# A feed-forward block's DRAM traffic split over two queues, with one operand stored already split

## The chip, the cores and the metric

The kernel runs on one core of one Trainium2 chip. The metric is the time of one execution on the device in microseconds (us). A core has five engines with an instruction list each: TensorE (in the profile PE, its weight loads PEld) multiplies matrices, VectorE (DVE) and ScalarE (ACT) work elementwise, GpSimd (POOL) does small work, and SyncE (SP) here only starts transfers. A transfer is put on the list of the engine that starts it; each list is worked through in its order, and all transfers run on the core's 16 DMA engines.

## The reference

Two layers over a sequence of 1024 tokens of width 1024, batch 1. Layer 0 is a retention and gated delta-net mixer, layer 1 a gated linear recurrence. After each mixer stands the feed-forward block that the change is about:

```
def conv_ffn(hn, w_up, conv_w, conv_b, w_down):      # hn: 1024 x 1024
    up = causal_dwconv(hn @ w_up, conv_w) + conv_b    # w_up: 1024 x 5632, 3 taps
    gate, val = jnp.split(up, 2, axis=-1)             # 2816 columns each
    return (jax.nn.silu(gate) * val) @ w_down         # w_down: 2816 x 1024
...
    h = h + conv_ffn(rms_norm(h, norm_ffn[layer]), ffn_w_up[layer], ffn_conv_w[layer],
                     ffn_conv_b[layer], ffn_w_down[layer])
```

Everything is in float32.

## The kernel before

Activations lie with channels on the 128 partitions and time along them. A float32 product is made of three matmuls (`mm3`, lines 319 to 321): each operand is split into a rounded part `hi` and a rest `lo`, and hi x hi, hi x lo and lo x hi are added up in PSUM. To split costs one ScalarE copy (`hi`) and one VectorE subtraction (`lo`).

The two large products of the feed-forward block use a two-by-two block scheme with seven products where the plain way has eight. `pair_product` makes product `o` (0 to 6) of a pair of output tiles from `kk` slices, three matmuls a slice: 12 matmuls for `kk` = 4. The seven right-hand operands are sums and differences of the blocks of the activations; I call them sets 0 to 6. The seven products share three PSUM banks (`BANK = "ACACABA"`), and after each product a VectorE addition reads the bank (`pair_sums` in the up projection, `pair_added`, line 820, in the down projection, where it adds to the residual `H`).

**Up projection.** 22 hidden tiles `p`, one after the other, each seven products against the sets of the block's input, which lie in `operand(0)` to `operand(6)`. When tile `p`'s products are done, `gate` and `hidden` convolve, gate and multiply on ScalarE and VectorE (lines 850, 852, 936, 941); the result `y` goes through `store_parts`. The hidden tiles fall into groups `c` = 0, 1, 2 of 8, 8 and 6 (`third`, true in layer 0 alone, says that the third group is treated like the others; in layer 1 tiles 16 to 21 are multiplied in the plain way by `final`). `store_parts` makes what the down projection needs from the tile: blocks that are operands as they are, and differences of blocks (`t1` to `t4`). A set in `whole[c]` is split at once (lines 877, 878) and goes to `p_dram` (in the profile `pf_dram`) as `hi` and `lo`; the others go to `s_dram` (`sf_dram`) raw.

**Down projection.** For each group `c` four tiles `t` of seven products. `load_set(c, o)` brings set `o` back into the place of an operand that is no longer used: a set of `whole[c]` in 2 `kk` transfers of 256 KB (line 914), a raw one in `kk` transfers (line 922) into half tiles taken in turn from `room[c]`, each then copied (line 924) and subtracted (line 925). `room[c]` has eight halves, of the buffer `R` and of three `t` tiles. The pool of `t` tiles has three buffers, so `room` waits until the last up tile's `t` tiles have been stored. Group 0's sets take the places of the up projection's operands, so set `o` can start when product `o` of the last up tile (21) is done: `after(21, o)` calls `load_set(0, o)`. Group 1's sets are fetched during the last tile of group 0 (`following`), group 2's during the last tile of group 1. Tile 21's own `hidden` comes after the third down tile of group 0.

The order on each engine is made by a planner from program order, its cost estimates and what waits for what; TensorE's order is fixed by hand only for the first two up tiles. Weights stream through SP too (line 292) into `raw` buffers and are split (lines 272, 273) as they are used.

Of the kernel before, what the change touches and what calls it, by code (L numbers as in the profile page):

```python
# [16 lines left out]
ALU = mybir.AluOpType  # L17
# [6 lines left out]
HALF = 512  # L24
# [65 lines left out]
def f32(ap):  # L90
    return ap.bitcast(F32)
# [12 lines left out]
class Block:  # L104
# [708 lines left out]
    def pair_added(self, t):  # L813

        V = self.nc.vector
        h = lambda i, j: self.H[2 * t + i].rearrange("p (h n c) -> p h n c", h=2, n=2)[:, :, j, :]
        to = ((0, 0), (1, 1), (0, 1), (0, 1), (1, 1), (0, 0), (1, 0))

        def sums(o, ps):
            V.tensor_tensor(h(*to[o]), ps.rearrange("p (h c) -> p h c", c=256), h(*to[o]), ALU.add)  # L820
        return sums

    def ffn(self, layer, gain):
        nc, I = self.nc, self.I
        V, A = nc.vector, nc.scalar
        third = gain is not None
        sets = 3 if third else 2
        y_dram = self.tc.dram_tile([NPAIR, P, T], F32, name=f"yf_dram{layer}")
        s_dram = self.tc.dram_tile([sets, 5, 4, P, HALF], F32, name=f"sf_dram{layer}")

        p_dram = self.tc.dram_tile([sets, 4, 4, 2, P, HALF], F32, name=f"pf_dram{layer}")
        if not third:
            l_dram = self.tc.dram_tile([NPAIR - 16, 2, P, T], F32, name=f"lf_dram{layer}")
        depth = lambda c: 4 if c < 2 else 3

        def where(c, o):

            if c == 0 or not third:
                return self.operand(o)
            if c == 1:  # L840
                return self.operand((o + 3) % 7)
            if o < 3:
                i = (20, 14, 26)[o]
                return self.slots1(i, 6).rearrange("p (s n c) -> p n s c", n=2, c=256)
            return self.s2[:, :, 6 * (o - 3):6 * (o - 2), :]
# [14 lines left out]
        whole = [{0: 0, 1: 1, 3: 2}] + 2 * [{0: 0, 1: 1, 3: 2, 5: 3}]  # L860
        room, loads = {}, [0, 0, 0]

        def store_parts(p, y, hi):

            hi = hi.bitcast(F32R)
            lo = self.parts.tile([P, T], F32R, tag="lo", name="lo")
            if p >= 16 and not third:
                self.split_half(y, (hi, lo))
                for e, t in enumerate((hi, lo)):
                    nc.sync.dma_start(l_dram[p - 16, e], f32(t))  # L870
                return
            c, k = divmod(p, 8)
            kk = depth(c)
            first = slice(0, HALF)

            def store_split(o, src, at):
                A.copy(halves(hi[:, at]), src)  # L877
                V.tensor_tensor(halves(lo[:, at]), src, f32(halves(hi[:, at])), ALU.subtract)  # L878
                for e, t in enumerate((hi, lo)):
                    nc.sync.dma_start(p_dram[c, whole[c][o], k % kk, e], f32(t[:, at]))  # L880
            store = lambda o, r: nc.sync.dma_start(s_dram[c, place[o], k % kk], r)
            sub = lambda out, a, b: V.tensor_tensor(halves(out), a, b, ALU.subtract)  # L882
# [10 lines left out]
            t4 = t3  # L893
            nc.sync.dma_start(halves(t3), blocks(y_dram[p - kk])[:, :, 1])
            nc.sync.dma_start(t2, s_dram[c, place[1], k - kk])
# [5 lines left out]
            sub(t4, v[:, :, 0], halves(t2))  # L901
            store(6, t4)
            if 5 in whole[c]:
                store_split(5, v[:, :, 0], slice(HALF, T))
            else:
                nc.sync.dma_start(halves(s_dram[c, place[5], k % kk]), v[:, :, 0])

        def load_set(c, o):

            x, kk = where(c, o), depth(c)  # L910
            if o in whole[c]:
                for k in range(kk):
                    for e in range(2):
                        nc.sync.dma_start(f32(x[:, :, kk * e + k, :]), halves(p_dram[c, whole[c][o], k, e]))
                return
            if c not in room:
                ts = [self.R] + [self.t() for _ in range(3)][::-1]
                room[c] = [t[:, i * HALF:(i + 1) * HALF] for i in range(2) for t in ts]
            for k in range(kk):
                r = room[c][loads[c] % 8]  # L920
                loads[c] += 1
                nc.sync.dma_start(r, s_dram[c, place[o], k])
                hi, lo = (x[:, :, e + k, :] for e in (0, kk))
                A.copy(hi, halves(r))
                V.tensor_tensor(lo, halves(r), f32(hi), ALU.subtract)  # L925
# [22 lines left out]
        def after(p, o):  # L948
            if p < NPAIR - 1:
                if o == 5:  # L950
                    tgs[p] = gate(p)
            elif o:
                for q in (0, 1) if o == 1 else (o,):
                    load_set(0, q)


        with self.tc.manual_schedule(engines={mybir.EngineType.PE}):
# [1005 lines left out]
```

## Time and profile before

| | |
|---|---|
| median of 3 runs | 2143.78 us (2143.31 to 2144.47) |
| the profiled execution | 2145.08 us, its span 2143.2 us |
| granted TensorE clock | 0.999 |
| instructions | 29749 |
| DMA moved | 313.23 MB, mean 146 GB/s |
| queue q1 (hardware; SP's transfers) | 304.15 MB, 42.5% of 16 engines |
| queue q0 (the transfers that GpSimd starts) | 0.81 MB, 0.2% |
| layer 0's feed-forward block | from about 575 to 1204 us, the down projection from about 985 |

Instructions are grouped by line of the kernel and by tile (`out<-in`, buffer numbers left out). A releaser behind `<-` is what ended an engine's idle time. Matmuls are pipelined: each is given from its start to its modelled end, and consecutive ones overlap. `SPq` rows are the issues of transfers on SP's list; how long a transfer takes to land is given apart. GpSimd's own issues are rows of POOL.

### The profile page before, as it was taken

The numbers are of one execution on the slowest core, as the hardware profiler recorded it, in microseconds if no ns is written. First come the engines' busy times: TensorE is split into PE (matmuls) and PEld (weight loads), VectorE is DVE, ScalarE is ACT, GpSimd is POOL, SyncE is SP. The second block draws the span as 40 slices with busy tenths as digits, with TensorE's granted clock in tenths as the row PEclk, the third lists the DMA queues.
The fourth block names the chain that finished last, engine by engine and source line by source line (L and its number), as shares of the span: only waits on it lengthen the run. The fifth ranks groups of instructions, "written<-read, shape, count | busy, mean of one in ns | idle before, by whom it ended". The sixth has DMA issues, their size and how long they took to land.

```text
span 2143.2 us, 29749 instructions
## 1 busy us (share of the span) xinstructions
PE 2127.4 (99%) x10648; PEld 1771.9 (83%) x10648; DVE 1722.2 (80%) x2630; ACT 1077.3 (50%) x1750; POOL 100.5 (5%) x115
## 2 busy tenths in 40 slices
PE   9999999999999999999999999999999999999998
PEld 7878888888888888887888888888888888888887
DVE  7995677776998989988868786768999889878645
ACT  6444423135665555555324576756655555554222
POOL 0102122300000000000000000000000000000002
PEclk9999999999999999999999999999999999999999
DMA  5354433543145435448745212142354445375542
GB/s 188 91 170 126 136 94 94 172 142 118 46 172 178 160 137 179 172 172 289 233 161 172 72 57 80 64 158 65 123 186 163 149 151 177 118 262 183 182 169 85
DMA packets 242021, 313.23 MB, mean 146 GB/s; under 512 B 62432, under 2 KB 129424, under 8 KB 241872
## 3 DMA queue, kind: packets, MB, share of 16 engines
q1 hardware_dynamic: 205632, 304.15, 42.5%
q10 hardware_dynamic: 35088, 6.36, 1.5%
q8 instruction: 84, 1.38, 0.3%
q0 software_dynamic: 1152, 0.81, 0.2%
q14 instruction: 65, 0.53, 0.1%
HBM read 215.79 MB, written 95.45 MB: 145 GB/s over the span
## 4 chain that ended last, share of the span: by engine, by line
PE 63%; issue 30%; DVE 3%; DMA 2%; POOL 1%; SPq 0%; ACT 0%; POOLq 0%; DVEq 0%
PE ps L319 19%; PE ps L320 18%; PE ps L321 18%; PE pc L319 1%; PE pc L321 1%; PE pc L320 1%; DMA s<-pf_dram 1%; DMA t<-sf_dram 0%; DVE wlo L273 0%; DVE l L1416 0%; DVE l L1418 0%; DVE h L1387 0%; PE pc L1551 0%; PE ps L1595 0%; PE pc L1663 0%
## 5 line engine op out<-in xcount | busy, mean ns | idle before, releaser
L319 PE MATMUL ps<-s,whi 128*128 128x512 f32 (+1 forms) x2692 | 1049.1, 391 | 1.5 <-DVE h L820 0.9
L320 PE MATMUL ps<-s,whi 128*128 128x512 f32 (+1 forms) x2692 | 1044.1, 388 | 2.1 <-DVE s L925 1.9
L321 PE MATMUL ps<-s,wlo 128*128 128x512 f32 (+1 forms) x2692 | 1042.7, 388 | 0.6 <-DVE wlo L273 0.6
L272 ACT CAST whi<-raw 128x512 fp32r<-128x512 f32 (+2 forms) x616 | 374.1, 613 | 611.9 <-PE ps L320 471.6
L319 PEld LDWEIGHTS ps<-s,whi 128*128 128x128 f32 x2692 | 505.8, 188 | 107.0 <-ACT whi L272 1.6
L320 PEld LDWEIGHTS ps<-s,whi 128*128 128x128 f32 x2692 | 505.9, 188 | 106.1 <-DVE s L925 4.6
L321 PEld LDWEIGHTS ps<-s,wlo 128*128 128x128 f32 x2692 | 505.6, 188 | 104.5 <-DVE wlo L273 1.4
L273 DVE TENSOR_TENSOR wlo<-raw,whi 128x512 fp32r<-128x512 f32 (+2 forms) x616 | 415.0, 680 | 50.8 <-ACT whi L272 42.3
L852 DVE SCALAR_TENSOR_TENSOR t<-halo,cols,t 128x1024 f32<-128x1024 f32 x176 | 221.6, 1281 | 2.4 <-ACT t L850 1.0
L820 DVE TENSOR_TENSOR h<-ps,h 128x512 f32<-128x512 f32 x140 | 96.3, 689 | 75.7 <-PE ps L321 75.5
L810 DVE TENSOR_TENSOR halo<-ps,kept 128x512 f32<-128x512 f32 (+1 forms) x138 | 91.8, 666 | 71.1 <-PE ps L321 70.5
L850 ACT ACTIVATE t<-halo,cols 128x1024 f32<-128x1024 f32 x88 | 109.5, 1247 | 18.0 <-DVE halo L810 9.0
L805 ACT COPY kept<-ps 128x512 f32<-128x512 f32 (+1 forms) x138 | 77.0, 558 | 11.0 <-PE ps L321 9.6
L472 POOL TENSOR_TENSOR rtok<-rtok,npow 128x4 f32<-128x4 f32 (+1 forms) x10 | 9.9, 990 | 1097.2 <-DVE rtok L471 1097.2
L877 ACT CAST t<-t 128x512 fp32r<-128x512 f32 x68 | 41.2, 621 | 39.1 <-DVE t L941 37.1
L941 DVE TENSOR_TENSOR t<-t 128x1024 f32<-128x1024 f32 x44 | 53.6, 1219 | 0.0
L553 DVE TENSOR_TENSOR h<-ps,h 128x512 f32<-128x512 f32 (+1 forms) x48 | 28.6, 599 | 30.6 <-PE ps L321 30.5
L882 DVE TENSOR_TENSOR t<-t 128x512 f32<-128x512 f32 x76 | 52.1, 686 | 0.6 <-DMA sf_dram<-t 0.6
L936 ACT ACTIVATE t<-t 128x1024 f32<-128x1024 f32 x44 | 46.8, 1063 | 10.4 <-DVE t L852 10.3
L407 ACT ACTIVATE t<-h 128x512 f32<-128x512 f32 (+1 forms) x49 | 26.9, 564 | 45.8 <-DVE h L553 43.8
L878 DVE TENSOR_TENSOR lo<-t 128x512 fp32r<-128x512 f32 x68 | 46.7, 686 | 0.0
L294 DVE TENSOR_TENSOR raw<-raw 128x512 f32<-128x512 f32 (+1 forms) x64 | 43.6, 681 | 3.3 <-issue 1.9
(341 smaller groups left out, 2170.7 us busy)
## 6 DMA issues: line engine op xcount, KB each, us to landing
raw<-in_ffn_up_dram SPq DMA_DIRECT2D x176, 256.0 KB, 2.7
s<-pf_dram SPq DMA_DIRECT2D x136, 256.0 KB, 5.2
sf_dram<-t SPq DMA_DIRECT2D x84, 256.0 KB, 2.4
pf_dram<-t SPq DMA_DIRECT2D x68, 256.0 KB, 2.6
pf_dram<-lo SPq DMA_DIRECT2D x68, 256.0 KB, 2.6
t<-sf_dram SPq DMA_DIRECT2D x67, 256.0 KB, 4.8
raw<-in_ffn_w_dram SPq DMA_DIRECT2D x64, 256.0 KB, 3.1
raw<-in_mix_in_dram SPq DMA_DIRECT2D x52, 256.0 KB, 3.0
```

The costliest lines, as they stand in the source:

```text
L272: self.nc.scalar.copy(hi[:, 0:w], raw[:, 0:w])
L273: eng.tensor_tensor(lo[:, 0:w], raw[:, 0:w], f32(hi[:, 0:w]), ALU.subtract)
L319: mm(ps, whi, xhi, start=start, stop=False)
L320: mm(ps, whi, xlo, start=False, stop=False)
L321: mm(ps, wlo, xhi, start=False, stop=stop)
L805: A.copy(kept[o], ps)
L810: V.tensor_tensor(dst(i, j), v(ps), v(kept[k]), ALU.add)
L820: V.tensor_tensor(h(*to[o]), ps.rearrange("p (h c) -> p h c", c=256), h(*to[o]), ALU.add)
L850: A.activation(t, buf[:, 2:2 + T], AF.Identity, scale=w(0), bias=self.col(f"ffn_cb{layer}", tile_i))
L852: V.scalar_tensor_tensor(t, buf[:, 2 + j:2 + j + T], w(j), t, ALU.mult, ALU.add)
L882: sub = lambda out, a, b: V.tensor_tensor(halves(out), a, b, ALU.subtract)
L941: V.tensor_tensor(tg, tg, tv, ALU.mult)
```

## The change

In layer 0 (`third`):

- The transfers that `store_parts` starts for tiles 16 to 21, stores and fetches, are started by GpSimd in place of SP.
- The fetches of raw pieces in `load_set` are started by GpSimd, for all three groups.
- Set 5 of group 0 joins `whole[0]`: tiles 4 to 7 store it split, and it comes back in eight transfers, with no copy and subtraction.
- Sets 4 and 6 of group 0 are no longer called for during up tile 21, but after the sums of products 0 and 2 of the first down tile, and `issue_after` puts the VectorE subtractions behind those sums on VectorE's list (the transfers and ScalarE copies are not tied).
- `room` is taken in another order: both halves of a tile follow each other.

In both layers the difference `t4` is written over a block of `y` that nothing reads any more, not over `t3`, and its store reads from there.

```
--- before.py
+++ after.py
@@ -817,7 +817,7 @@
         to = ((0, 0), (1, 1), (0, 1), (0, 1), (1, 1), (0, 0), (1, 0))
 
         def sums(o, ps):
-            V.tensor_tensor(h(*to[o]), ps.rearrange("p (h c) -> p h c", c=256), h(*to[o]), ALU.add)
+            return V.tensor_tensor(h(*to[o]), ps.rearrange("p (h c) -> p h c", c=256), h(*to[o]), ALU.add)
         return sums
 
     def ffn(self, layer, gain):
@@ -857,17 +857,18 @@
         halves = lambda ap: ap.rearrange("p (n c) -> p n c", n=2)
         place = {1: 0, 4: 1, 2: 2, 6: 3, 5: 4}
 
-        whole = [{0: 0, 1: 1, 3: 2}] + 2 * [{0: 0, 1: 1, 3: 2, 5: 3}]
+        whole = [{0: 0, 1: 1, 3: 2, **({5: 3} if third else {})}] + 2 * [{0: 0, 1: 1, 3: 2, 5: 3}]
         room, loads = {}, [0, 0, 0]
 
         def store_parts(p, y, hi):
 
+            queue = nc.gpsimd if third and p >= 16 else nc.sync
             hi = hi.bitcast(F32R)
             lo = self.parts.tile([P, T], F32R, tag="lo", name="lo")
             if p >= 16 and not third:
                 self.split_half(y, (hi, lo))
                 for e, t in enumerate((hi, lo)):
-                    nc.sync.dma_start(l_dram[p - 16, e], f32(t))
+                    queue.dma_start(l_dram[p - 16, e], f32(t))
                 return
             c, k = divmod(p, 8)
             kk = depth(c)
@@ -877,8 +878,8 @@
                 A.copy(halves(hi[:, at]), src)
                 V.tensor_tensor(halves(lo[:, at]), src, f32(halves(hi[:, at])), ALU.subtract)
                 for e, t in enumerate((hi, lo)):
-                    nc.sync.dma_start(p_dram[c, whole[c][o], k % kk, e], f32(t[:, at]))
-            store = lambda o, r: nc.sync.dma_start(s_dram[c, place[o], k % kk], r)
+                    queue.dma_start(p_dram[c, whole[c][o], k % kk, e], f32(t[:, at]))
+            store = lambda o, r: queue.dma_start(s_dram[c, place[o], k % kk], r)
             sub = lambda out, a, b: V.tensor_tensor(halves(out), a, b, ALU.subtract)
             v = blocks(y)
             t = self.t()
@@ -890,20 +891,20 @@
                 store_split(1, halves(t1), slice(HALF, T))
                 return
             t3, t2 = t[:, 0:HALF], t[:, HALF:]
-            t4 = t3
-            nc.sync.dma_start(halves(t3), blocks(y_dram[p - kk])[:, :, 1])
-            nc.sync.dma_start(t2, s_dram[c, place[1], k - kk])
+            t4 = v[:, :, 1]
+            queue.dma_start(halves(t3), blocks(y_dram[p - kk])[:, :, 1])
+            queue.dma_start(t2, s_dram[c, place[1], k - kk])
             store_split(3, v[:, :, 1], first)
             sub(t3, v[:, :, 1], halves(t3))
             store(4, t3)
             sub(t2, v[:, :, 1], halves(t2))
             store(2, t2)
-            sub(t4, v[:, :, 0], halves(t2))
-            store(6, t4)
+            V.tensor_tensor(t4, v[:, :, 0], halves(t2), ALU.subtract)
+            queue.dma_start(halves(s_dram[c, place[6], k % kk]), t4)
             if 5 in whole[c]:
                 store_split(5, v[:, :, 0], slice(HALF, T))
             else:
-                nc.sync.dma_start(halves(s_dram[c, place[5], k % kk]), v[:, :, 0])
+                queue.dma_start(halves(s_dram[c, place[5], k % kk]), v[:, :, 0])
 
         def load_set(c, o):
 
@@ -914,12 +915,17 @@
                         nc.sync.dma_start(f32(x[:, :, kk * e + k, :]), halves(p_dram[c, whole[c][o], k, e]))
                 return
             if c not in room:
-                ts = [self.R] + [self.t() for _ in range(3)][::-1]
-                room[c] = [t[:, i * HALF:(i + 1) * HALF] for i in range(2) for t in ts]
+                ts = [self.t() for _ in range(3)]
+                half = lambda t, i: t[:, i * HALF:(i + 1) * HALF]
+                if third:
+                    room[c] = [half(t, i) for t in (self.R, ts[1], ts[2], ts[0]) for i in range(2)]
+                else:
+                    room[c] = [half(t, i) for i in range(2) for t in [self.R] + ts[::-1]]
             for k in range(kk):
+                queue = nc.gpsimd if third else nc.sync
                 r = room[c][loads[c] % 8]
                 loads[c] += 1
-                nc.sync.dma_start(r, s_dram[c, place[o], k])
+                queue.dma_start(r, s_dram[c, place[o], k])
                 hi, lo = (x[:, :, e + k, :] for e in (0, kk))
                 A.copy(hi, halves(r))
                 V.tensor_tensor(lo, halves(r), f32(hi), ALU.subtract)
@@ -951,7 +957,8 @@
                     tgs[p] = gate(p)
             elif o:
                 for q in (0, 1) if o == 1 else (o,):
-                    load_set(0, q)
+                    if not third or q not in (4, 6):
+                        load_set(0, q)
 
 
         with self.tc.manual_schedule(engines={mybir.EngineType.PE}):
@@ -969,13 +976,17 @@
         following = {0: {1: (4, 5), **{o: ((o + 4) % 7,) for o in range(2, 7)}},
                      1: {2: (0,), 3: (1, 2), 4: (3,), 5: (4,), 6: (5, 6)}}
         plain = {0: {1: (0, 1), **{o: (o,) for o in range(2, 7)}}, 1: {}}
+        set_at = lambda *at: at in ((0, 0, 0), (0, 0, 2))
         for c in range(sets):
             done = self.down_steps(gain) if c == 2 else {}
             for t in range(4):
                 sums, banks = self.pair_added(t), {}
                 key = (f"ffn_w{layer}", c, t) if c < 2 else (f"ffn_v{layer}", t)
                 for o in range(7):
-                    sums(o, self.pair_product(banks, o, self.quarter(key, o), x=where(c, o)))
+                    last = sums(o, self.pair_product(banks, o, self.quarter(key, o), x=where(c, o)))
+                    if third and set_at(c, t, o):
+                        with self.tc.issue_after(last.ins):
+                            load_set(0, 4 if o == 0 else 6)
                     if t == 3 and c < 2:
                         for q in (following if third else plain)[c].get(o, ()):
                             load_set(c + 1, q)
```

More of the change, by code (lines that the diff above doesn't have):

```diff
@@ L819, in sums @@
         def sums(o, ps):
-            V.tensor_tensor(h(*to[o]), ps.rearrange("p (h c) -> p h c", c=256), h(*to[o]), ALU.add)
+            return V.tensor_tensor(h(*to[o]), ps.rearrange("p (h c) -> p h c", c=256), h(*to[o]), ALU.add)
         return sums
@@ L858, in ffn @@
         place = {1: 0, 4: 1, 2: 2, 6: 3, 5: 4}
-        whole = [{0: 0, 1: 1, 3: 2}] + 2 * [{0: 0, 1: 1, 3: 2, 5: 3}]
+        whole = [{0: 0, 1: 1, 3: 2, **({5: 3} if third else {})}] + 2 * [{0: 0, 1: 1, 3: 2, 5: 3}]
         room, loads = {}, [0, 0, 0]
         def store_parts(p, y, hi):
+            queue = nc.gpsimd if third and p >= 16 else nc.sync
             hi = hi.bitcast(F32R)
@@ L869, in store_parts @@
                 for e, t in enumerate((hi, lo)):
-                    nc.sync.dma_start(l_dram[p - 16, e], f32(t))
+                    queue.dma_start(l_dram[p - 16, e], f32(t))
                 return
@@ L879, in store_split @@
                 for e, t in enumerate((hi, lo)):
-                    nc.sync.dma_start(p_dram[c, whole[c][o], k % kk, e], f32(t[:, at]))
-            store = lambda o, r: nc.sync.dma_start(s_dram[c, place[o], k % kk], r)
+                    queue.dma_start(p_dram[c, whole[c][o], k % kk, e], f32(t[:, at]))
+            store = lambda o, r: queue.dma_start(s_dram[c, place[o], k % kk], r)
             sub = lambda out, a, b: V.tensor_tensor(halves(out), a, b, ALU.subtract)
@@ L892, in store_parts @@
             t3, t2 = t[:, 0:HALF], t[:, HALF:]
-            t4 = t3
-            nc.sync.dma_start(halves(t3), blocks(y_dram[p - kk])[:, :, 1])
-            nc.sync.dma_start(t2, s_dram[c, place[1], k - kk])
+            t4 = v[:, :, 1]
+            queue.dma_start(halves(t3), blocks(y_dram[p - kk])[:, :, 1])
+            queue.dma_start(t2, s_dram[c, place[1], k - kk])
             store_split(3, v[:, :, 1], first)
@@ L900, in store_parts @@
             store(2, t2)
-            sub(t4, v[:, :, 0], halves(t2))
-            store(6, t4)
+            V.tensor_tensor(t4, v[:, :, 0], halves(t2), ALU.subtract)
+            queue.dma_start(halves(s_dram[c, place[6], k % kk]), t4)
             if 5 in whole[c]:
@@ L905, in store_parts @@
             else:
-                nc.sync.dma_start(halves(s_dram[c, place[5], k % kk]), v[:, :, 0])
+                queue.dma_start(halves(s_dram[c, place[5], k % kk]), v[:, :, 0])
         def load_set(c, o):
@@ L916, in load_set @@
             if c not in room:
-                ts = [self.R] + [self.t() for _ in range(3)][::-1]
-                room[c] = [t[:, i * HALF:(i + 1) * HALF] for i in range(2) for t in ts]
+                ts = [self.t() for _ in range(3)]
+                half = lambda t, i: t[:, i * HALF:(i + 1) * HALF]
+                if third:
+                    room[c] = [half(t, i) for t in (self.R, ts[1], ts[2], ts[0]) for i in range(2)]
+                else:
+                    room[c] = [half(t, i) for i in range(2) for t in [self.R] + ts[::-1]]
             for k in range(kk):
+                queue = nc.gpsimd if third else nc.sync
                 r = room[c][loads[c] % 8]
                 loads[c] += 1
-                nc.sync.dma_start(r, s_dram[c, place[o], k])
+                queue.dma_start(r, s_dram[c, place[o], k])
                 hi, lo = (x[:, :, e + k, :] for e in (0, kk))
@@ L953, in after @@
                 for q in (0, 1) if o == 1 else (o,):
-                    load_set(0, q)
+                    if not third or q not in (4, 6):
+                        load_set(0, q)
         with self.tc.manual_schedule(engines={mybir.EngineType.PE}):
@@ L971, in ffn @@
         plain = {0: {1: (0, 1), **{o: (o,) for o in range(2, 7)}}, 1: {}}
+        set_at = lambda *at: at in ((0, 0, 0), (0, 0, 2))
         for c in range(sets):
@@ L977, in ffn @@
                 for o in range(7):
-                    sums(o, self.pair_product(banks, o, self.quarter(key, o), x=where(c, o)))
+                    last = sums(o, self.pair_product(banks, o, self.quarter(key, o), x=where(c, o)))
+                    if third and set_at(c, t, o):
+                        with self.tc.issue_after(last.ins):
+                            load_set(0, 4 if o == 0 else 6)
                     if t == 3 and c < 2:
```

## Prediction

> **What bounds the kernel now.** I read the busy times first, then stretches of the run, then the matmuls one by one where TensorE paused, then what the DMA queue did there.
>
> ```profile
> PE 2127.4 (99%) x10648; PEld 1771.9 (83%) x10648; DVE 1722.2 (80%) x2630; ACT 1077.3 (50%) x1750; POOL 100.5 (5%) x115
> ...
> 575.00:984.00 409.00, 409.00 (x1844) 340.18 (x1843) 371.85 (x499) 235.28 (x348) 0.00 (x0) 1.00 0.48 167
> 984.00:1066.00 82.00, 78.92 (x338) 62.49 (x338) 67.61 (x105) 35.80 (x57) 0.00 (x0) 1.00 0.74 250
> 1066.00:1142.00 76.00, 76.00 (x336) 62.51 (x335) 50.26 (x81) 21.88 (x37) 0.00 (x0) 1.00 0.60 204
> 1142.00:1204.00 62.00, 61.08 (x270) 50.32 (x269) 55.12 (x97) 33.50 (x62) 0.00 (x0) 1.00 0.36 116
> ```
>
> The columns of a stretch are its length, then busy us (and instructions) of TensorE, its weight load, VectorE, ScalarE and GpSimd, the granted clock, the DMA engines' busy share and GB/s. The change adds or removes no matmul, so it can gain only where TensorE stands still. TensorE is busy 99% of the span, and most of the change lives in the feed-forward block of layer 0. There TensorE is idle for 82.00 - 78.92 = 3.08 us behind 984 us, where the down projection begins, and for 0.92 us behind 1142 us, and nowhere else. The 3.08 us are eight pauses, five of them ended by the split at L925. These are the matmuls (start, duration, and in brackets the idle time before and its releaser); two of the eight, alike, are left out:
>
> ```profile
> 990.09 0.50 PE L320 MATMUL ps<-s,whi 128*128 128x512 f32 x1 [0.21 <-DMA s<-pf_dram]
> ...
> 998.78 0.50 PE L319 MATMUL ps<-s,whi 128*128 128x512 f32 x1 [0.55 <-ACT s L924]
> 999.61 0.50 PE L320 MATMUL ps<-s,whi 128*128 128x512 f32 x1 [0.33 <-DVE s L925]
> 1002.02 0.39 PE L321 MATMUL ps<-s,wlo 128*128 128x512 f32 x1
> 1002.25 0.39 PE L319 MATMUL ps<-s,whi 128*128 128x512 f32 x1
> 1003.12 0.50 PE L320 MATMUL ps<-s,whi 128*128 128x512 f32 x1 [0.48 <-DVE s L925]
> 1003.46 0.40 PE L321 MATMUL ps<-s,wlo 128*128 128x512 f32 x1
> 1006.62 0.50 PE L320 MATMUL ps<-s,whi 128*128 128x512 f32 x1 [0.48 <-DVE s L925]
> 1008.58 0.39 PE L319 MATMUL ps<-s,whi 128*128 128x512 f32 x1
> 1009.82 0.50 PE L321 MATMUL ps<-s,wlo 128*128 128x512 f32 x1 [0.62 <-DVE wlo L273]
> ...
> 1151.02 0.39 PE L321 MATMUL ps<-s,wlo 128*128 128x512 f32 x1
> 1152.33 0.47 PE L319 MATMUL ps<-s,whi 128*128 128x512 f32 x1 [0.92 <-DVE h L820]
> 1152.63 0.40 PE L320 MATMUL ps<-s,whi 128*128 128x512 f32 x1
> ```
>
> Undisturbed, starts are 0.23 us apart (1002.02 to 1002.25), though each lasts 0.39: they overlap. A pause therefore costs more than its idle time. From 1002.25 over 1003.12 to 1003.46 two steps take 1.21 instead of 0.46: 0.75 lost for 0.48 idle, 0.27 more. So the eight pauses cost 3.08 + 8 x 0.27 = 5.2 us, and the one at 1152.33 costs 1.31 + 0.30 - 0.46 = 1.15 us. All that can be won is 6.4 us, 0.30% of the run. Comparisons of this kernel resolve about 0.2%, here 4.3 us.
>
> Why the pauses? The operands come back from DRAM in this stretch:
>
> ```profile
> 971.00:1004.00 33.00, 31.02 (x130) 23.51 (x129) 23.02 (x37) 15.50 (x27) 0.00 (x0) 1.00 1.00 354
> 980.00:985.00 5.00, 5.00 (x24) 4.14 (x23) 4.06 (x7) 1.47 (x3) 0.00 (x0) 1.00 0.80 261
> 1000.00:1005.00 5.00, 4.52 (x20) 3.40 (x19) 4.49 (x8) 4.81 (x9) 0.00 (x0) 1.00 1.05 400
> 1060.00:1080.00 20.00, 20.00 (x88) 16.13 (x88) 9.38 (x15) 4.98 (x8) 0.00 (x0) 1.00 1.08 382
> 1140.00:1145.00 5.00, 5.00 (x24) 4.14 (x23) 4.06 (x7) 2.08 (x4) 0.00 (x0) 1.00 0.99 314
> ...
> 980.39 0.32 SPq L881 DMA_DIRECT2D sf_dram<-t  x1
> 980.77 4.46 SPq L914 DMA_DIRECT2D s<-pf_dram  x7
> 985.28 1.54 SPq L922 DMA_DIRECT2D t<-sf_dram  x3
> ...
> 979.67 0.69 DVE L882 TENSOR_TENSOR t<-t 128x512 f32<-128x512 f32 x1 [0.60 <-DMA sf_dram<-t]
> 998.11 1.91 ACT L924 CAST s<-t 128x512 fp32r<-128x512 f32 x3 [5.49 <-DMA t<-sf_dram]
> 1005.27 0.69 DVE L820 TENSOR_TENSOR h<-ps,h 128x512 f32<-128x512 f32 x1 [0.41 <-PE ps L321]
> 1005.88 1.89 DVE L925 TENSOR_TENSOR s<-t,s 128x512 fp32r<-128x512 f32 x3
> ```
>
> Two causes are mixed. One is order: SP works its list in turn, so the raw pieces (985.28) stand behind seven split ones (980.77), these behind the last store of the tile before (980.39), and that behind a sum that itself waited 0.60 us for a DMA (979.67). On VectorE a ready split (1005.88) stands behind a sum that waits for TensorE (1005.27), and TensorE then waits for the split (1006.62). The other is volume: from 971 to 1004 us the DMA engines' share is 1.00; 33 us at 354 GB/s are 11.7 MB. No order removes that part.
>
> **The change, part by part.**
>
> *Set 5 stored split.* In the up projection, tiles 4 to 7 each get one more ScalarE copy and one more VectorE subtraction (0.64 and 0.63 us, from the threes at 998.11 and 1005.88) and one more store. The cover is VectorE's slack:
>
> ```profile
> 694.00:713.00 19.00, 19.00 (x86) 15.72 (x85) 17.07 (x24) 10.33 (x16) 0.00 (x0) 1.00 0.50 166
> 846.00:865.00 19.00, 19.00 (x85) 15.75 (x84) 17.68 (x25) 10.77 (x16) 0.00 (x0) 1.00 0.51 174
> ```
>
> The first row has such a tile; the second has tiles 12 to 15, which carry this split already, 17.68 us of 19 and no pause. So 0; uncovered it would be 4 x 0.63 = 2.5 us. At the start of the down projection it removes four copies and four splits, but fetches eight pieces of 256 KB instead of four: 1.05 MB more, in the full stretch. At 354 GB/s that is 3.0 us more of transfer.
>
> *GpSimd's queue.* 42 stores and fetches of tiles 16 to 21 and 33 fetches of raw pieces (12, 12 and 9 for the three groups) leave SP. SP can then issue set 0, 1, 3 and 5 as TensorE frees their places, without the waits at 980. The price of GpSimd's own issue has only these rows:
>
> ```profile
> L1437 POOL DMA_DIRECT2D l<-t_dram x32 | 17.7, 555 | 84.9 <-DMA t_dram<-l 52.5 <-PE pc L1466 17.0 <-ACT l L1448 14.2
> DMA to landing us min/median/max: 1.6/2.2/3.3
> 182.10 1.10 POOL L1437 DMA_DIRECT2D l<-t_dram  x2 [1.67 <-ACT l L1448]
> 182.25 0.69 DVE L273 TENSOR_TENSOR wlo<-raw,whi 128x512 fp32r<-128x512 f32 x1 [5.92 <-ACT whi L272]
> ```
>
> 75 x 0.555 us = 42 us on an engine that does nothing from 575 to 1204 us; a VectorE subtraction beside two such issues (182.25) takes the usual 0.69. So no direct cost: 0, at worst the 1.1 us between the usual landing, 2.2, and the slowest, 3.3, once, for a store that frees a buffer.
>
> What does the stream then need? 11.7 + 1.05 = 12.75 MB from 971 us. At the best row, 400 GB/s, it ends at 1002.9; at the mean of now, 354, at 1007.0; at 314, the slowest row with a share near 1, at 1011.6. I take 382, the row 1060 to 1080: it is the nearest, mostly split pieces in one unbroken run from SP, which is what SP will now do, while today's 354 holds the gap of 0.80 at 980. That gives 971 + 33.4 = 1004.4.
>
> The first down tile ends at 1008.58 (the next one's first matmul), after seven pauses that cost 5.2 - 0.9 = 4.3; the eighth, 0.62 + 0.27 = 0.9, is the same backlog in the next tile. Unpaused it would end at 1004.3. If set 5 lands last, 12 matmuls of the seventh product (2.7) and the last three of the sixth (0.7) still follow: 1004.4 + 3.4 = 1007.8, a loss of 3.5 in place of 5.2, gain 1.7. If the seventh set, raw, lands last, then copy 0.64, split 0.63 and 0.7 follow: 1006.4, gain 3.1. I take 1.7: SP has 8.4 MB of sets to bring, GpSimd 2.6, so the longer list ends last.
>
> *Splits behind sums.* The subtractions of sets 4 and 6 are queued behind the sums of products 0 and 2. A sum must be done before the product after next uses its bank again; behind a sum there are always 2.7 us. Four splits, 4 x 0.63 = 2.5, fit between a sum and that. If their data is late, the next sum waits behind them, as at 1152.33 today; that is inside the range from 1.7 down.
>
> *The last sum over a dead block.* The wait of 0.60 at 979.67 goes. It is not on TensorE's path by itself; it lets one store leave earlier. In layer 1 the edit is the same; 0.
>
> *The third group, 1142 us.*
>
> ```profile
> 1144.50 0.48 SPq L922 DMA_DIRECT2D R<-sf_dram  x1
> 1149.89 0.62 ACT L924 CAST s<-R 128x512 fp32r<-128x512 f32 x1 [2.19 <-DMA R<-sf_dram]
> 1150.42 0.56 DVE L294 TENSOR_TENSOR raw<-raw 128x384 f32<-128x384 f32 x1 [1.90 <-issue]
> 1150.90 0.68 DVE L925 TENSOR_TENSOR s<-R,s 128x512 fp32r<-128x512 f32 x1
> ```
>
> One raw piece is last in SP's list, lands near 1149.8, and its split (1150.90) delays the sum for which TensorE waits. By GpSimd it goes early. Of 1.15 us I take 1.0; 0 if the weight sum at 1150.42 alone holds VectorE. At the seam of 1060 to 1080, share 1.08 and no idle time, raw pieces may now overtake split ones: up to 3 x 0.69 (256 KB at 382) = 2.1 lost; they can also use earlier slack, so 0.
>
> *Sum:* 1.7 + 1.0 = 2.7 us. The profiled execution took 2145.08 (span 2143.2), so 2142.4 by its own time; it stands 1.3 above the median of the runs, 2143.78, which becomes 2141.1.
>
> **Rivals.** *All pauses go:* all 5.2 and 1.15, 2137.4. For it: five pauses name VectorE's split, an order that the edits address. Against it: the stream would have to end by about 1001, 425 GB/s, above any row. With 400 GB/s it is 3.1 + 1.0, 2139.7. *Volume eats the order:* the stream stays at 354, ends at 1007.0, the tile at 1010.4: 6.1 lost for 5.2, +0.9 - 1.0, 2143.7, no change. For it: share 1.00 already. [...] *Slower:* two queues of short rows run at the slow row's 314 GB/s; the stream ends at 1011.6, the tile at 1015.0, 10.7 lost for 5.2: +5.5 - 1.0, 2148.3. It decides from 353 GB/s downward, where the stream ends after 1007.1 and more than 5.2 + 1.0 is lost; from 316, an end at 1011.4, the loss is over 4.3 us. Against it: only mixed stretches with SP's list interrupted run so slowly; the unbroken one has 382.
>
> **How the numbers follow.** Partial relief as summed 0.46 (2139.5 to 2143.0); all or nearly all pauses gone, from 2139.5 down, 0.24; volume eats it 0.23; slower by the slow stream 0.07. The range 2137.3 to 2145.0 leaves out the slow stream and the tails; the likeliest case alone has 2139.5 to 2143.0. Faster by over 0.2% (under 2139.5) is the second case, 0.24; slower (over 2148.1) the last, 0.07; the rest, 0.69, is within 0.2%.
>
> **What will show it.** Right: near 985 SP issues split pieces without a gap, the DMA share stays above 1.0 until about 1004, the pauses named by the split at L925 go, and what is left is a wait for a split piece's DMA in the sixth product (set 5). The 1152 pause is gone. Wrong: pauses in the up projection (a late GpSimd store holds a buffer), sums waiting behind splits, or no pause left at all.

## The result, and the profile after

The changed kernel takes 2155.69 us, median of four runs (2154.71 to 2156.92), against 2143.55 (2142.87 to 2144.47) for the kernel before beside it: a ratio of 1.0057, 95% interval 1.0039 to 1.0074, 12.1 us slower. The prediction was 2141.1 with a range to 2145.0. The profiled execution took 2154.71 (span 2152.6), 9.6 more than the profiled one of before.

Where is it? At the last sums of the up projection the kernel after is even 1.8 us ahead (981.16 against 982.92), and behind the third seam the two run alike to the end. Nearly all is lost at the places where a group's operands come back, called seams here: the first behind 984 us, the second behind 1060, the third behind 1140. The stretches of the kernel after (columns as in the prediction; the number ahead of the DMA share is the granted clock of TensorE):

```profile
985.00:990.00 5.00, 4.28 (x19) 3.19 (x18) 0.69 (x1) 1.22 (x2) 2.38 (x5) 1.00 1.07 403
990.00:995.00 5.00, 1.00 (x3) 0.83 (x4) 3.13 (x6) 4.73 (x10) 1.08 (x2) 0.76 1.05 407
995.00:1000.00 5.00, 5.00 (x14) 3.94 (x13) 4.18 (x7) 3.64 (x5) 0.00 (x0) 0.56 1.07 385
1000.00:1005.00 5.00, 5.00 (x23) 4.11 (x22) 2.20 (x5) 0.62 (x1) 1.08 (x2) 1.00 1.07 406
1005.00:1010.00 5.00, 3.47 (x15) 2.57 (x15) 5.00 (x9) 1.24 (x2) 1.29 (x2) 1.00 0.47 170
...
1070.00:1075.00 5.00, 2.59 (x8) 0.97 (x6) 0.94 (x2) 0.08 (x1) 0.27 (x1) 0.95 1.06 401
1075.00:1080.00 5.00, 4.67 (x10) 2.65 (x10) 1.29 (x2) 0.62 (x1) 0.00 (x0) 0.50 1.09 384
1080.00:1085.00 5.00, 5.00 (x20) 4.00 (x20) 0.83 (x2) 0.00 (x0) 0.00 (x0) 0.87 1.09 383
```

The kernel before in two of these stretches:

```profile
990.00:995.00 5.00, 4.50 (x16) 2.94 (x17) 2.80 (x5) 1.86 (x3) 0.00 (x0) 1.00 1.07 379
...
1075.00:1080.00 5.00, 5.00 (x23) 3.89 (x22) 0.69 (x1) 0.00 (x0) 0.00 (x0) 1.00 1.08 391
```

Two things are new. TensorE stands still longer (3 matmuls in 990 to 995 where before had 16), and at both seams the granted clock falls to half: 14 and 10 matmuls fill five microseconds that hold 22 or 23 otherwise (rows of 995 and 1075, clock 0.56 and 0.50). Neither was there before, where every such row has 1.00. The trace's record of the granted clock has 0.5 from 992.59 to 999.42 and from 1074.51 to 1081.34, 6.83 us each time. The first fall lies inside the stand itself, which ends at 994.00.

TensorE's matmuls at the first seam (start, duration, idle time before and its releaser):

```profile
988.66 0.39 PE L320 MATMUL ps<-s,whi 128*128 128x512 f32 x1
988.89 0.39 PE L321 MATMUL ps<-s,wlo 128*128 128x512 f32 x1
994.00 0.77 PE L319 MATMUL ps<-s,whi 128*128 128x512 f32 x1 [4.72 <-DVE h L820]
994.57 0.63 PE L320 MATMUL ps<-s,whi 128*128 128x512 f32 x1
994.99 0.63 PE L321 MATMUL ps<-s,wlo 128*128 128x512 f32 x1
995.42 0.63 PE L319 MATMUL ps<-s,whi 128*128 128x512 f32 x1
...
999.57 0.40 PE L320 MATMUL ps<-s,whi 128*128 128x512 f32 x1
999.81 0.40 PE L321 MATMUL ps<-s,wlo 128*128 128x512 f32 x1
```

It waits 4.72 us for a sum, and the matmuls behind it start 0.43 us apart instead of 0.23. Why is the sum late? VectorE's list, then ScalarE's, then GpSimd's (fetches of raw pieces are now L928, the copy and subtraction of a split L930 and L931), then SP's:

```profile
989.04 0.69 DVE L931 TENSOR_TENSOR s<-t,s 128x512 fp32r<-128x512 f32 x1 [6.59 <-ACT s L930]
990.06 0.69 DVE L931 TENSOR_TENSOR s<-t,s 128x512 fp32r<-128x512 f32 x1 [0.32 <-ACT s L930]
992.56 0.69 DVE L273 TENSOR_TENSOR wlo<-raw,whi 128x512 fp32r<-128x512 f32 x1 [1.81 <-ACT whi L272]
993.17 0.69 DVE L820 TENSOR_TENSOR h<-ps,h 128x512 f32<-128x512 f32 x1
...
988.39 0.62 ACT L930 CAST s<-t 128x512 fp32r<-128x512 f32 x1 [6.84 <-DMA t<-sf_dram]
...
990.91 0.62 ACT L930 CAST s<-t 128x512 fp32r<-128x512 f32 x1 [0.27 <-DMA t<-sf_dram]
...
991.91 0.62 ACT L272 CAST whi<-raw 128x512 fp32r<-128x512 f32 x1
...
983.08 3.36 POOL L928 DMA_DIRECT2D t<-sf_dram  x6 [3.63 <-DMA sf_dram<-t]
986.43 0.55 POOL L928 DMA_DIRECT2D R<-sf_dram  x1
...
965.28 32.61 SPq L915 DMA_DIRECT2D s<-pf_dram  x32
998.09 48.72 SPq L292 DMA_DIRECT2D raw<-in_ffn_w_dram  x16
```

The sum of product 0 (993.17) stands behind two splits of set 2 and a weight split, and the weight split (992.56) waits 1.81 us for its ScalarE copy (991.91), which stands behind two copies of set 4 (the second at 990.91). In the kernel before that sum ran ahead of set 2's splits:

```profile
987.65 0.69 DVE L820 TENSOR_TENSOR h<-ps,h 128x512 f32<-128x512 f32 x1 [1.55 <-PE ps L321]
...
991.37 1.33 DVE L925 TENSOR_TENSOR s<-t,s 128x512 fp32r<-128x512 f32 x2 [2.42 <-ACT s L924]
```

The splits wait for pieces that GpSimd could fetch only at 983.08, after 3.63 us for the last tile's stores to land. And the six fetches of 983.08 hold four of set 4, which the change meant to hold behind that very sum (the fetch of 986.43 is set 6's first, as early): its hold sets the place of the subtractions in VectorE's list alone, while ScalarE copies set 4's pieces as they come and GpSimd, with nothing ahead of the fetches, issues them at once.

The second seam has another wait (TensorE's waits from 1060 to 1090 us: in total, times, longest), with GpSimd's fetches for the third group beside it:

```profile
PE ps L319 <- DMA s<-pf_dram: 2.5, 2, 1.3
...
1061.04 1.08 POOL L928 DMA_DIRECT2D t<-sf_dram  x2 [0.81 <-DVE s L931]
1066.64 1.22 POOL L928 DMA_DIRECT2D R<-sf_dram  x2 [4.52 <-DVE s L931]
1069.20 1.07 POOL L928 DMA_DIRECT2D t<-sf_dram  x2 [1.34 <-DVE s L931]
...
1053.77 28.50 SPq L915 DMA_DIRECT2D s<-pf_dram  x32
```

To set kernels side by side I add up, at each seam of a profiled execution, by how much each step from one matmul's start to the next exceeds 0.227 us (steps over 0.24 us alone, in 984 to 1020, 1060 to 1092 and 1140 to 1172). Before: 5.6 + 0.2 + 1.2 = 6.9 us. After: 9.5 + 7.0 + 1.1 = 17.5, so 10.6 more, against 9.6 in the profiled times. Some 13 matmuls at half clock at each seam, 0.20 each, are by this estimate 5.2 of the 10.6; the rest is standing still.

### The profile page after: what moved, and what is told of

It reads as the page before. It is cut to its first block, busy times and chain, and to the rows that moved or that the text cites. A ratio compares the mean times of both kernels' runs of the same rounds, so it can differ in the third digit from the quotient of the medians.

```text
span 2152.6 us, 29843 instructions
## 1 busy us (share of the span) xinstructions
PE 2131.1 (99%) x10648; PEld 1774.2 (82%) x10648; DVE 1720.9 (80%) x2630; ACT 1075.7 (50%) x1750; POOL 142.3 (7%) x190
## 4 chain that ended last, share of the span: by engine, by line
PE 65%; issue 31%; DMA 2%; DVE 1%; POOL 1%; ACT 0%; SPq 0%; POOLq 0%; DVEq 0%; ACTq 0%
PE ps L319 19%; PE ps L320 19%; PE ps L321 18%; DMA s<-pf_dram 1%; PE pc L319 1%; PE pc L320 1%; PE pc L321 1%; PE ps L1654 0%; PE ps L1656 0%; PE ps L1655 0%; PE pc L1562 0%; PE ps L1606 0%; PE pc L1674 0%; PE ps L1704 0%; PE pc L1588 0%
## 5 line engine op out<-in xcount | busy, mean ns | idle before, releaser
L805 ACT COPY kept<-ps 128x512 f32<-128x512 f32 (+1 forms) x138 | 77.0, 558 | 11.1 <-PE ps L321 9.6
L942 ACT ACTIVATE t<-t 128x1024 f32<-128x1024 f32 x44 | 46.8, 1063 | 10.6 <-DVE t L852 10.5
L379 DVE TENSOR_TENSOR halo<-ps,R 128x512 f32<-128x512 f32 x36 | 24.6, 686 | 27.4 <-PE ps L321 25.5
L319 PE MATMUL ps<-s,s 128*128 128x256 f32 (+1 forms) x144 | 46.0, 320 | 0.0
```

The lines of the kernel that those rows point to most:

```text
L319: mm(ps, whi, xhi, start=start, stop=False)
L805: A.copy(kept[o], ps)
```

## The experiments

Each ratio is to the kernel before on the same chip, whose medians there were 2144.4 to 2144.9 (2143.55 for the first row); seams are the sums just defined.

| kernel | median us | ratio, 95% interval | seams 1, 2, 3 (us) | longest step |
|---|---|---|---|---|
| after | 2155.69 | 1.0057 (1.0039 to 1.0074) | 9.5, 7.0, 1.1 | 5.11 |
| e1_all_sp | 2146.84 | 1.0009 (1.0000 to 1.0018) | 7.7, 0.6, 0.4 | 0.97 |
| e2_hold_set2 | 2155.56 | 1.0053 (1.0038 to 1.0068) | 10.3, 6.4, 1.4 | 6.56 |
| e3_group3_sp | 2150.78 | 1.0032 (1.0019 to 1.0045) | 11.1, 2.0, 0.7 | 4.96 |
| e4_both | 2151.82 | 1.0033 (1.0021 to 1.0046) | 10.2, 1.3, 0.5 | 6.50 |
| e5_real_wait | 2150.08 | 1.0026 (1.0015 to 1.0037) | 10.8, 2.3, 0.5 | 5.98 |
| e6_loads_sp | 2146.91 | 1.0009 (0.9999 to 1.0019) | 7.7, 0.4, 0.1 | 3.48 |
| e7_sp_set5_raw | 2143.66 | 0.9993 (0.9984 to 1.0003) | 4.8, 0.7, 0.7 | 1.16 |
| v_set5_split | 2145.91 | 1.0008 (0.9999 to 1.0017) | 6.9, 0.6, 1.6 | 1.71 |
| b3_set3_raw | 2142.07 | 0.9987 (0.9977 to 0.9996) | 2.9, 0.6, 0.5 | 0.74 |
| b4_e7_set3_raw | 2142.74 | 0.9992 (0.9983 to 1.0001) | 3.2, 0.4, 0.6 | 0.82 |
| b5_sets13_raw | 2143.82 | 0.9995 (0.9986 to 1.0004) | 5.6, 0.6, 1.2 | 2.88 |

**All on SP again (e1_all_sp).**

```
-            queue = nc.gpsimd if third and p >= 16 else nc.sync
+            queue = nc.sync
...
-                queue = nc.gpsimd if third else nc.sync
+                queue = nc.sync
```

> The changed kernel with every transfer back on SP's list; set 5 split, the dead block, the room's order and the splits behind two sums stay. Theory A (the second list lets the planner put set 2's copies and splits ahead of the first sum, and lets group 2's raw pieces start some 15 us early into a full stretch): both seams recover, 2141 to 2146, no pause over 2 us and no stretch of half clock. Rival B (the added 1.05 MB of set 5 and the new order of room and splits are the loss, not the queue): it stays over 2150. Rival C (only GpSimd's larger packets starve SP's) also says 2141 to 2146 here; the next kernels separate it from A.

It came out at 2146.84: of some 12 us lost, all but about 2.3 (by the interval 0 to 3.9) is the second queue's. There is no half clock (every row of the first two seams has 1.00), and the second seam is whole again.

**Set 2's last pieces behind the sum as well (e2_hold_set2).** The step that looked like the culprit, the sum behind splits, taken away. The ScalarE copies are tied behind the weight copies too.

```
-                        load_set(0, q)
+                        load_set(0, q, (0, 1) if third and q == 2 else None)
...
-                        with self.tc.issue_after(last.ins):
+                        with self.tc.issue_after(last.ins), self.tc.issue_after(self.last_hi.ins):
+                            if o == 0:
+                                load_set(0, 2, (2, 3))
```

> The changed kernel with the last two pieces of set 2 tied too: subtractions behind the first down tile's first sum, ScalarE copies (of sets 2 and 4, and 6 behind its own) behind the weight copies already called for. All transfers stay with GpSimd. Theory A: the 4.9 us pause at 994 and the half clock behind it (about 2.7 us) go, smaller pauses of 1 to 3 us in all take their place; the seam at 1070 keeps its loss; 2148 to 2151. Rival C (SP's pieces are starved whoever waits): the first seam keeps 8 us or more, 2154 to 2156.

Theory A missed and rival C had the range: 2155.56, 11.1 us over the kernel before beside it, next to nothing won. The sum ran on time, and TensorE stood still all the same, 3.4 us later and longer (6.56 us from 992.28). VectorE's first sum, and TensorE's waits from 985 to 1012 us:

```profile
987.27 0.69 DVE L820 TENSOR_TENSOR h<-ps,h 128x512 f32<-128x512 f32 x1 [1.56 <-PE ps L321]
...
PE ps L319 <- DMA s<-pf_dram: 6.2, 1, 6.2
PE ps L319 <- DVE h L820: 0.7, 1, 0.7
```

Now product 3 waits 6.2 us for the split pieces of set 3. So the sum behind the splits was only the first of two waits, one covering the other. From 987 to 993 us the kernel after moved 1.90 MB by GpSimd's queue (463 packets of 4096 bytes) and 0.58 MB by SP's (563 packets of 1024 bytes), counted in the trace's packet records. In packets the two are near each other; in bytes GpSimd's queue has 77%, and the pieces of sets 2, 4 and 6 come in ahead of set 3, which is wanted before sets 4 and 6. No run started the raw fetches from an engine other than these two, so how much is owed to the longer packets and how much to a second queue as such stays open.

**The third group's raw pieces on SP (e3_group3_sp, and e4_both with e2's hold).**

```
-                queue = nc.gpsimd if third else nc.sync
+                queue = nc.gpsimd if third and c < 2 else nc.sync
```

> The changed kernel with the third group's nine raw pieces (c = 2) fetched by SP again; all else as changed. Theory A: of the loss at the second seam (about 7 us with its half clock) nearly all goes, the first seam keeps its 4.9 us pause; 2148 to 2150. Rival C: group 1's own four pieces of set 2 and its packets still starve SP's, the seam keeps 4 us or more; 2152 to 2156.

> Both edits of the two kernels before together, queue of GpSimd otherwise kept. Theory A: no half clock at either seam, 2140 to 2145, the effects of the two add. Rival C: over 2148.

e3 is 6.3 us over its kernel before, where the kernel after is 12.1 over; the second seam's sum fell from 7.0 to 2.0, its half clock is gone. The intervals of the two kernels just overlap, so it is the trace that carries the reading: the pieces fetched a whole group early, into a full stretch (a DMA share of 1.05 to 1.09 from 1060 to 1085 us in the kernel after), were the second seam's loss. e4 missed theory A's 2140 to 2145 as e2 had missed its range: at the first seam TensorE waits 6.1 us for `s<-pf_dram`. Of the theories in these texts, the one that puts the first seam's loss down to the place of the sum in the list falls with e2 and e4; that GpSimd's fetches starve SP's split pieces stands (TensorE's waits for them of 6.2 us in e2 and 6.1 in e4).

**The fetches held in fact (e5_real_wait).** On e4's base; `behind` is one column of the block that a sum has written:

```
+                if behind is not None:
+                    V.tensor_copy(r[:, 0:1], behind)
                 queue.dma_start(r, s_dram[c, place[o], k])
...
-                            load_set(0, 4 if o == 0 else 6)
+                    if third and (c, t, o) in ((0, 0, 2), (0, 0, 4)):
+                        with self.tc.issue_after(last.ins):
+                            load_set(0, o + 2, None, self.H[o // 4][:, 256:257])
```

> e4_both with set 4's and set 6's fetches made to wait in fact: a one-column copy of the summed block into each staged tile stands ahead of the fetch that overwrites it, after sum 2 (set 4) and sum 4 (set 6), so GpSimd's queue can't issue them at 984 us. Theory of shares (GpSimd's fetches take bytes from SP's split pieces of set 3, for which TensorE stood 6.2 us in e2 and 6.1 us in e4): set 4's 1.05 MB no longer lands ahead of set 3's, at the 400 GB/s of that stretch 2.6 us; the pause ahead of product 3 falls to 3 to 4 us and the time to 2148 to 2150. Theory of lists (the place of sums and splits in VectorE's list is all that counts): no less than e4's 2151.8, since nothing of the lists' order that mattered there is moved. What both can't say: whether set 4 then comes late itself, by its own 1.05 MB.

The time, 2150.08, stands at the upper edge of the range of the theory of shares, and its interval overlaps e4's, so the time alone decides nothing. The trace does (GpSimd's list; TensorE's, then ScalarE's waits from 985 to 1012 us; here L929 is the one-column copy, L930 the fetch, L932 and L933 the copy and subtraction of a split):

```profile
993.56 1.14 POOL L930 DMA_DIRECT2D t<-sf_dram  x2 [9.09 <-DVE t L929]
...
PE ps L319 <- ACT s L932: 5.5, 1, 5.5
PE ps L320 <- DVE s L933: 0.2, 1, 0.2
...
ACT whi L272 <- DMA raw<-in_ffn_w_dram: 11.2, 1, 11.2
```

Set 4's first fetches wait until 993.56, and the wait for set 3 is gone: the early pieces of sets 4 and 6 had made set 3 late. But a third wait of 5.5 us takes its place. Set 4's copy stands in ScalarE's list behind a weight copy that waits 11.2 us, because SP brings the weights after all 32 split pieces. Behind each wait that is taken away the wait of the next product comes to light.

**Stores on GpSimd, fetches on SP (e6_loads_sp).**

```
-                queue = nc.gpsimd if third else nc.sync
+                queue = nc.sync
```

> The changed kernel with the fetches of the raw pieces back on SP's queue and the last tiles' stores and small fetches left on GpSimd's. Theory of shares: the stores cost nothing (they lie in the up phase, ahead of the full stretch), so the time is that of e1, 2145 to 2148, no pause over 2 us at 985 to 1010, no half clock. Rival (GpSimd's stores land later, 2.9 to 3.7 us against 2.4, and hold the first fetches back): 2150 or more, with a wait for sf_dram<-t of 3 us ahead of the first fetch.

2146.91, as with everything on SP: the stores cost nothing that these runs resolve, the fetches of raw pieces are the loss by the queue. One expectation missed: there is one step of 3.48 us at 1001.18 (a wait of 3.1 us for ScalarE's split), with 3.41 us of half clock; its seam costs no more than e1's many small pauses.

**Set 5 raw or split (e7_sp_set5_raw, v_set5_split).**

```
# e7, on e1
-        whole = [{0: 0, 1: 1, 3: 2, **({5: 3} if third else {})}] + 2 * [{0: 0, 1: 1, 3: 2, 5: 3}]
+        whole = [{0: 0, 1: 1, 3: 2, }] + 2 * [{0: 0, 1: 1, 3: 2, 5: 3}]
# v, on the kernel before
-        whole = [{0: 0, 1: 1, 3: 2}] + 2 * [{0: 0, 1: 1, 3: 2, 5: 3}]
+        whole = [{0: 0, 1: 1, 3: 2, **({5: 3} if third else {})}] + 2 * [{0: 0, 1: 1, 3: 2, 5: 3}]
```

> e1 (both queues SP's) with set 5 of the first group raw again, as in the kernel before: what is left of the change is the last sum over the dead block, the order of the staged halves and the splits held behind two sums. Theory of volume (set 5's split adds 1.05 MB to the full stretch, 2.6 us at 400 GB/s, part of it hidden): 2143 to 2145, e1's excess of 2.3 us gone. Rival (the held splits or the order of the halves cost it): 2146 to 2148 as e1.

> The kernel before with one part of the change alone: set 5 of the first group stored split. Theory of volume (1.05 MB more in the full stretch, and from e1 to e7 3.2 us): 2146 to 2149 where before has 2144 to 2145. Rival (removing four late splits from VectorE's list pays for it, as the prediction had it): 2143 to 2145.

e7 stands 1.2 us under its kernel before, e1 2.3 over its own: set 5's split costs some 3.6 us there. Alone on the kernel before it costs 1.5, somewhat under what was expected, its interval from 0.2 less to 3.6 more (0.0017 of 2144). What is left of the change in e7 is worth between 3.4 us won and 0.6 lost: nothing shown.

**The volume turned the other way (b3_set3_raw, b4_e7_set3_raw, b5_sets13_raw).** On the kernel before, set 3 of the first group raw instead of set 5 split (b4 the same on e7; b5 drops `1: 1` there as well):

```
...
-        place = {1: 0, 4: 1, 2: 2, 6: 3, 5: 4}
+        place = {1: 0, 4: 1, 2: 2, 6: 3, 5: 4, 3: 5}
-        whole = [{0: 0, 1: 1, 3: 2}] + 2 * [{0: 0, 1: 1, 3: 2, 5: 3}]
+        whole = [{0: 0, 1: 1, **({} if third else {3: 2})}] + 2 * [{0: 0, 1: 1, 3: 2, 5: 3}]
...
-            store_split(3, v[:, :, 1], first)
+            if 3 in whole[c]:
+                store_split(3, v[:, :, 1], first)
+            else:
+                nc.sync.dma_start(halves(s_dram[c, place[3], k % kk]), v[:, :, 1])
```

> The kernel before with the volume turned the other way: set 3 of the first group is stored raw too, and split when fetched, so 1.05 MB less is stored late in the up phase and fetched in the full stretch, and ScalarE and VectorE get four splits more (4 x 0.62 and 4 x 0.69 us). Theory of volume: the stream ends 2.6 us earlier, the pauses of 5.3 us at the first seam fall by 1 to 2.6 us, 2141 to 2142.5. Rival (the splits' place in the lists is what holds TensorE there): four more splits ahead of sums, 2143.5 to 2147.

> The version that should beat both: e7 (all on SP, set 5 raw, last sum over the dead block, order of the halves and held splits of the change) with set 3 of the first group raw too, as in b3. If e7's 1.2 us under before and b3's 2.8 add up: 2140.5 to 2142. If the stretch has no pause left to take (b3 had 0.6 us of waits there): as b3, 2141.5 to 2142.5.

> b3 with set 1 of the first group raw too: 1.05 MB less again, four more copies and splits, eight staged halves for five raw sets. Theory of volume: b3 has waits of 0.6 us left at this seam, so at most 1 us better, 2141 to 2142.5. Rival (the splits now fill VectorE, 4.7 to 5.0 of 5 us in b3's stretches from 990 on, and set 1 is wanted first): worse than b3 by 1 to 4 us, with waits for the split.

b3 takes 2142.07, a ratio of 0.9987 (0.9977 to 0.9996): 2.8 us under the kernel before beside it, in the range of the theory of volume. It is the lowest ratio found and the only one whose interval lies under 1. One such interval among twelve kernels is weak alone, but its first seam agrees: 2.9 us where before has 5.6. TensorE's waits from 980 to 1165 us add up to 0.9 us (0.4, 0.3 and 0.2). Two rows of its first seam fit that:

```profile
990.00:995.00 5.00, 4.59 (x18) 3.01 (x17) 4.74 (x8) 4.80 (x9) 0.00 (x0) 1.00 0.98 365
1000.00:1005.00 5.00, 4.74 (x18) 2.84 (x16) 4.89 (x9) 4.53 (x8) 0.00 (x0) 1.00 1.00 360
```

The DMA share is 0.98 and 1.00, where before had 1.07 and 1.05, and VectorE has 4.7 to 4.9 us of work in 5: the two look to be in balance. b5 goes past it. With set 1 raw too, TensorE waits 2.5 us for a split's copy, the clock falls to half for 3.41 us (0.66 in the row 995 to 1000), and no gain shows any more (0.9995, no change), as its rival said. b4 (0.9992) adds e7's edits to b3 and shows no gain over it.

**Pauses by hand (p_doses, p_doses2).** Added to the kernel before, single runs of 2147.94 and 2164.16:

```
+                    extra = {(True, 1, 1): 7, (True, 1, 2): 10, (False, 0, 2): 13, (False, 1, 1): 16}   # p_doses
+                    extra = {(True, 1, 2): 20, (False, 0, 2): 17, (False, 1, 1): 24}                    # p_doses2
+                    for _ in range(extra.get((third, c, t), 0) if o == 2 else 0):
+                        spare = self.kept.tile([P, HALF], F32, tag="kept", name="kept")
+                        V.tensor_copy(spare, ps)
```

> The kernel before with pauses put in by hand where no transfer is full: behind the sum of product 2, VectorE copies the same bank 7 times (first group's successor, tile 1 of group 2), 10 times (tile 2), and in layer 1 13 and 16 times, so that TensorE has to wait for VectorE for growing times. Theory of the clock (a TensorE pause of some 3 us or more is followed by 6.83 us at half clock, whatever made the pause): the short pauses leave the matmuls 227 ns apart, the long ones are followed by about 16 matmuls 427 ns apart and a granted clock of 0.5 for 6.83 us, with the DMA engines not full. Rival (the half clock comes from the full DMA engines or from GpSimd's queue): no matmuls 427 ns apart at any of the four places. With 16 copies of 0.6 us the wait is at most 9.6 us; what slack the banks leave will show.

> p_doses with more copies: 20 behind the sum of product 2 of tile 2 of the second group in layer 0, 17 and 24 in layer 1 (first group tile 2, second group tile 1); nothing is fetched by GpSimd there and no stretch is near full. In p_doses 16 copies (9.65 us) gave a matmul gap of 2122 ns and no half clock, so a copy more adds some 0.6 us to the gap: 17, 20 and 24 should give some 2.7, 4.5 and 6.9 us. Theory of the clock: the two longer gaps are each followed by 6.83 us at half clock (matmuls 427 ns apart); the shortest stands near the bound and may fall either way. Rival (the half clock needs the full DMA engines or GpSimd's queue): none at any of the three.

p_doses misjudged the slack: the four doses gave steps of 2.12 us at most, and no half clock, which alone told nothing. p_doses2 settles it (matmuls, L983 being the added copies; then the stretches around the first pause, around the shortest, and inside the longest):

```profile
1121.09 0.39 PE L320 MATMUL ps<-s,whi 128*128 128x512 f32 x1
1125.60 0.79 PE L319 MATMUL ps<-s,whi 128*128 128x512 f32 x1 [4.13 <-DVE kept L983]
1126.19 0.63 PE L320 MATMUL ps<-s,whi 128*128 128x512 f32 x1
1126.62 0.63 PE L321 MATMUL ps<-s,wlo 128*128 128x512 f32 x1
...
1975.36 0.50 PE L319 MATMUL ps<-s,whi 128*128 128x512 f32 x1 [2.55 <-DVE kept L983]
1975.70 0.40 PE L320 MATMUL ps<-s,whi 128*128 128x512 f32 x1
...
1120.00:1125.00 5.00, 1.47 (x7) 0.89 (x5) 5.00 (x10) 0.00 (x0) 0.00 (x0) 0.89 0.67 210
1125.00:1130.00 5.00, 4.40 (x10) 3.47 (x11) 5.00 (x9) 1.14 (x2) 0.00 (x0) 0.50 0.13 39
...
1975.00:1980.00 5.00, 4.19 (x17) 3.11 (x17) 5.00 (x9) 1.66 (x3) 0.00 (x0) 1.00 0.97 312
...
2035.00:2040.00 5.00, 0.00 (x0) 0.00 (x0) 5.00 (x9) 0.00 (x0) 0.00 (x0) 0.87 0.00 0
```

Steps of 4.51 and 6.91 us each come with 6.83 us of half clock, beside DMA shares of 0.67 and 0.13 at the one and 0.00 in the other, and with no fetch by GpSimd; one of 2.94 us, beside a share of 0.97, comes with none. So at these two the half clock came without full DMA engines and without GpSimd's queue: copies on VectorE alone made TensorE stand still there.

## Why the prediction was wrong, step by step

*GpSimd's queue* is the step that failed. Its cost was put at 0, at worst 1.1 us; the raw fetches on it cost some 10. The queue was priced by its issues (75 x 0.555 us on an idle engine: GpSimd's busy time rose from 100.5 to 142.3 us and e6 shows the stores at no cost) and by the end of the stream. That end was near: 1004.4 foretold, and the row 1000 to 1005 is full, the next has 0.47. But what filled it last were weights, for SP's last fetch of split pieces, issued at 997.36, had landed by 1002.9, and no product waited for set 5; so the agreement is in part luck. The step took for granted that TensorE waits only for what comes last, in the sixth product. The two queues kept no common order here: sets 4 and 6, issued by GpSimd from 983.08 to 991.7, overtook set 3 for product 3, and the splits for set 2 came late before that. With the raw fetches back on SP (e6) 2.0 us over the kernel before are left of 12.1.

*Splits behind sums* said that four splits fit between two sums and that late data would hold up a sum. The second half happened, 4.7 us of it, but by the splits of set 2, which the change does not hold, and by set 4's copies on ScalarE, which it does not hold either; and a hold moves a place in a list, not a transfer. It was still not the price of the change, since e2 without that wait lost as much.

*Set 5 stored split* had the volume right: 3.0 us of transfer, against 1.5 alone and about 3.6 in e1 and e7, each known to some 2 or 3 us. What should have paid for it, the order, never did: e1, with all else of the change but the queue, has 7.7 us at the first seam where before has 5.6.

*The third group.* The raw pieces overtaking split ones at the second seam were named and put at up to 2.1 us, then taken as 0. The seam lost 6.8 us, and e3 gives 5.8 of the run's 12.1 back. The gain of 1.0 at 1152 did not come either: 1.1 us is lost there, as 1.2 before. In e3, with those pieces on SP again, it is 0.7, so no help of the queue shows.

*The last sum over a dead block* at 0 agrees with e7, as far as that resolves.

*The cost of a pause*, idle time and 0.27 us, held up to the step of 2.12 us in p_doses (1.73 of it idle, lost 2.0). At the seams of the kernel after the half clock was missing from the sum, by the estimate above 5.2 of 10.6 us. Of the rivals the slower one had the right sign, but by a slow stream of 314 GB/s; the stream ran at 383 to 407 and the loss came by order. The DMA engines' share did not rise with a second queue: 1.07 in 990 to 995 before, 1.05 after. The time of the rival by volume, 2143.7, did not come either, for the second queue cost order besides (e6).

Of the signs that the prediction set itself, two of being right came: a share above 1.0 until about 1004 and no more pauses at the subtraction of a split in the first seam. What should have been left, a wait in the sixth product, did not come, nor did the 1152 pause go; and a sign of being wrong, a sum waiting behind splits, did come.

## What to carry to other kernels

With the DMA engines full (shares of 1.04 to 1.07 from 980 to 1005 us in the kernel after), one queue in the order of need was worth some 10 us more here than two that each ran ahead (12.1 us over the kernel before with two, 2.0 with the raw fetches on SP): look at which operand each next product wants, not at when the last byte lands, and hold a transfer by data it must wait for, not by its place in a list. In such a stretch of this kernel bytes were the currency: 1.05 MB less of them, against four more copies and splits, gave 2.8 us (b3: raw and split later), so balance them against the engines that can make the data. Then read the clock's column: in the table below, steps of TensorE of 2.88 us and more, all but the one of 2.94, and several of 0.56 to 2.10 us within 5 to 6 us, came with 3.41 or 6.83 us at half speed.

## What the runs showed of the hardware

The half clock was not expected. Steps between matmul starts, and the time at half clock that began in them or just behind, by the trace's record:

| step us | kernel, at us | half clock us |
|---|---|---|
| 2.12 | p_doses, 2026.88 | none |
| 2.94 | p_doses2, 1975.36 | none |
| 2.88 | b5_sets13_raw, 995.86 | 3.41 |
| 3.21 and 3.48 | e3, 1011.25; e6, 1001.18 | 3.41 each |
| 4.96 | e3, 995.67 | 3.41 |
| 4.51, 5.11, 5.98 | p_doses2; after; e5 | 6.83 each |
| 6.50 to 6.91 | e4, e2, p_doses2 | 6.83 each |
| 0.66, 1.74, 0.56, 1.58, 0.70 within 6 us | after, second seam | 6.83 |
| 1.25, 0.84, 2.10 within 5 us | e2, second seam | 3.41 |

It lasted 3.41 or 6.83 us each time. In the 3.41 us ahead of the two falls in the kernel after, at 992.59 and 1074.51, TensorE was busy for 0.10 and 1.66 us, by the profile's modelled ends: one long step came ahead of the first, several short ones ahead of the second. The length of a step alone does not order the table: 2.88 us in b5 came with a fall, 2.94 in p_doses2 with none, and why is not shown.

The second is the share of the full DMA engines: from 987 to 993 us in the kernel after, GpSimd's queue moved 463 packets of 4096 bytes and SP's 563 of 1024, 77% of the bytes by GpSimd's.
